# Query packing from PSUM, a transferred key copy and a joined value product in a hybrid decoder step

## The chip, the cores and the metric

One Trainium2 chip; the kernel runs on one of its cores. The metric is the device time of one execution in microseconds (us), as the median of several runs. An execution is also recorded by the hardware profiler; its trace gives every instruction's start and duration on the engines: PE (TensorE matmul), PEld (its weight loads), DVE (VectorE), ACT (ScalarE), POOL (GpSimd) and SP (SyncE, which issues the DMA transfers here).

## The reference, cut to what matters

One inference step of a decoder trunk: dilated sliding-window attention (layer 0 here), a pooling mixer, and a gated convolution feed-forward after each. The change touches the attention of the 1024 prompt tokens only. There are three groups of 16 heads with dilation 1, 4 and 16; in each residue stream a query attends to itself and the 128 keys before it.

```python
def banded_attention(q, k, v, bias):
    ...
    s = jnp.einsum("nbqhd,nbkhd->nbhqk", qb, kb).astype(jnp.float32) * SCALE
    s = s + bias[:, np.clip(rel, 0, SPAN)]
    s = jnp.where(valid[None, :, None], s, NEG_INF)
    m = jnp.max(s, axis=-1)
    p = jnp.exp(s - m[..., None])
    l = jnp.sum(p, axis=-1)
    o = jnp.einsum("nbhqk,nbkhd->nbqhd", p.astype(v.dtype), vb).astype(jnp.float32)
```

All of it is float32. The kernel gets there with the float32r matmul: each operand is split into a high part (rounded to float32r) and a low part (the rest), and a product is the sum of high by high, high by low and low by high.

## The kernel before, in words

The attention stage works through 24 units, `order` (L794): head pair `hp` 0 to 7, and in each the groups `g` 2 (dilation 16), 1, 0. A unit's projection is 9 groups of 24 matmuls of 336 to 352 columns (3 operands `which` = q, k, v by 3 token chunks `c`), `accumulate` (L111). They are written to two PSUM banks in turn (tile `mm`, `bufs=2`), and `evacuate` (L356) empties a bank with one ACT instruction (L364) into the tile `raw` (tag `raw`, 3 buffers: q, k, v), in the order of the group's residue streams, so that for g of 1 and 2 the writes are strided.

While unit n is projected, the attention of unit n-1 is worked off beside it. `attend` (L803) puts its steps on a list with due places on a `clock` that ticks once per 3 matmuls (`between`, L834), 72 ticks to a unit: `scores` i at 6i+1, `probs_t` i at 6i+15, `pv` i at 6i+24, `finish_o` at 6i+26 for odd i, `transpose_v` at 4 and 28. Everything that is due is issued at once, to queues that each engine works off strictly in order. Extra tasks come along every 6 ticks: `Merge` (weights of the three groups, `weights` L558 and `rows` L575) and `Sample` (the 8 sample tokens; its cache loads and POOL products).

Two packing steps prepare scores of the unit under projection. `pack_q` (L386, at ticks 29, 32, 44.5, 46.5) fills the tiles `queries` for two heads h: high part on the head's own 64 partitions, low part on the other 64. `pack_k` (L400, at ticks 50, 53, 56, 59) fills `keys`: high part on both halves of the partitions, low part on the own half. Head 0 uses ACT and POOL, head 1 DVE alone, for the queries; for the keys DVE makes the own copy (L404), ACT the other (L405), and POOL or DVE the low part (L406). A score is then one product of `queries` with each of the two planes of `keys`.

`probs_t` transposes the probabilities into the PSUM bank `pt` (1 buffer), ACT takes the high part (L475) and DVE the low part (L476) into `phl`. `pv_mm` (L479) multiplies: for each head, `v` high and low side by side (128 stationary columns) by the high, then by the low probabilities (L485), four matmuls of 128 columns per step for g = 2, accumulated in one bank of tile `o` (3 buffers). ACT (L504) brings one half of the partitions over, DVE (L521) adds the halves.

Weights for every stage are 128x1024 tiles that are split by ACT (L95) and POOL (L96). After the attention stage a projection and two feed-forward layers follow; the change does not touch them, nor the norm code, but the norm's tiles at the start (`place`, L295) share the tag `p` with the probabilities.

Of the kernel before, what the change touches and what calls it, by code (L numbers as in the profile page):

```python
# [18 lines left out]
T, NS = 1024, 8  # L19
# [8 lines left out]
TAB = 384  # L28
RAW = 3

# [15 lines left out]
def trunk(ctx: ExitStack, tc: tile.TileContext, a, out):  # L46
# [231 lines left out]
    with ExitStack() as ph:  # L278
        qp = ph.enter_context(tc.tile_pool(name="qkv", bufs=1))
        mmp = ph.enter_context(tc.tile_pool(name="mmp", bufs=1, space=PSUM))  # L280
        app = ph.enter_context(tc.tile_pool(name="app", bufs=1, space=PSUM))
        sample_cols = [qp.tile([128, 3, 8, NS], F32, name=f"{x}s") for x in "qkv"]
        units = {}
# [4 lines left out]
        keys = [qp.tile([128, 2, T], F32R, name=f"k{h}") for h in range(2)]  # L288

        def load_x(c):  # L290
            c0, c1 = CHUNKS[c]
            for k in range(8):
                nc.sync.dma_start(out=xT[k][:, c0:c1], in_=a["x"][:, k, c0:c1])

        def place(kind, j=0, c=0):  # L295
            if kind in ("row", "square"):
                return qp.tile([128, 512], F32, name="nrow", tag="p", bufs=4)
            if kind == "acc":
                return part[:, j, CHUNKS[c][0]:CHUNKS[c][1]]
# [24 lines left out]
        def tables():  # L324

            def step(g, tag, src):
# [6 lines left out]
                else:  # L333
                    bs = qp.tile([16, 512], F32, name="bs", tag="p", bufs=4)[:, :136]
                    nc.vector.tensor_copy(bs, ps)
# [20 lines left out]
        def evacuate(u, which, ps, c):  # L356
# [24 lines left out]

        A, B = slice(0, 64), slice(64, 128)

        queries = []

        def pack_q(u):  # L386

            raw = u.raw[0]
            if not queries:
                queries.extend(x_row(h, F32R)[:, :T] for h in range(2))  # L390
# [7 lines left out]
            return parts(part, (0, T // 2))  # L398
# [12 lines left out]

        def parts(f, starts):
            return [partial(f, h, own, other, slice(t, t + T // 2)) for t in starts
                    for h, (own, other) in enumerate(((A, B), (B, A)))]

# [16 lines left out]
        def transpose_v(u, half):  # L432
            ps = app.tile([128, 4, 2, 64], F32, name="vt", tag="misc")
            for j in range(4):
                i = 4 * half + j
                nc.tensor.transpose(ps[:, j].rearrange("p a d -> p (a d)"),  # L436
                                    u.raw[2][:, T - 128 * i - 128:T - 128 * i], ident)
            v = qp.tile([128, 4, 2, 128], F32R, name="vhl", tag="vhl", bufs=2)
            nc.scalar.activation(v[:, :, :, 0:64], ps, AF.Copy)
            nc.vector.tensor_sub(v[:, :, :, 64:128], ps, v[:, :, :, 0:64].bitcast(F32))  # L440
            u.v[half] = v

        def scores(u, i):
# [3 lines left out]
            ps = app.tile([128, 2, 2, 128], F32, name="s", tag="s")  # L447
            p = qp.tile([128, 2, 256], F32, name="p", tag="p", bufs=4)
            if w == 128:
                for h in range(2):  # L450
                    nc.tensor.matmul(ps[:, h], queries[h][:, q], keys[h][:, :, k], start=True, stop=True)  # L451
                nc.vector.tensor_add(p[:, :, :w], ps[:, :, 0], u.bias[:, :, :w])
                s, bias = ps[:, :, 1], p
            else:
                s, bias = ps.rearrange("p h a q -> p h (a q)"), u.bias
                for h in range(2):
                    for x in range(2):
                        nc.tensor.matmul(s[:, h], queries[h][:, q], keys[h][:, x, k], start=x == 0, stop=x == 1)  # L458
            for h in range(2):
# [29 lines left out]
        def pv(u, j):  # L489
            first = j % 2 == 0  # L490
            if first:
                u.o = app.tile([128, 2, 256], F32, name="o", tag="o", bufs=3)
                if j and u.pt[j - 1][1] == 256:
# [3 lines left out]
            if j % 2:  # L497

                x = 256 * (j // 2 % 2)
                tmp = (part[:, 0, x:x + 256] if (u.hp, u.g) != order[23] else  # L500
                       qp.tile([128, 256], F32, name="ot", tag="ot", bufs=1))
                u.tmp = tmp, u.o
                for h, (own, other) in enumerate(((A, B), (B, A))):
                    nc.scalar.activation(tmp[own], u.o[other, h], AF.Copy)  # L504

        def finish_o(u, i):
# [13 lines left out]
            for h, own in enumerate((A, B)):  # L520
                nc.vector.tensor_add(dst[own], split(o[own, h]), split(tmp[own]))  # L521

# [17 lines left out]
        class Merge:  # L540
# [43 lines left out]
            def fetch(self, g):  # L584
                if self.hp < 7:
                    cb = x_row(2)[:, :T]
                else:
                    cb = qp.tile([128, NT], F32, name="cb", tag="raw", bufs=RAW)[:, :T]
                self.cb[g] = cb
# [307 lines left out]
        for n, (hp, g) in enumerate(order):  # L897
# [9 lines left out]
            for i, (which, c) in enumerate(seq):  # L907
                if which == len(wt):
                    wt.append(None if (n, i) == (0, 2) else w_get())
                    u.raw.append(qp.tile([128, NT], F32, name="raw", tag="raw", bufs=RAW))  # L910
                    if n:
# [38 lines left out]
                if i == 6 and n:  # L950
                    load_bias(u)
                if n and i in (2, 5):
                    places = (29, 29 + 3, 44.5, 44.5 + 2) if i == 2 else [50 + 3 * j for j in range(4)]
                    plan.extend(zip(places, pack_q(u) if i == 2 else pack_k(u)))
                    plan.sort(key=lambda x: x[0])
                if n == 0 and i == 5:
                    for f in tables() + [partial(load_bias, u)]:
                        later(f, .8)
                if n == 0 and i in (6, 7):
                    nc.scalar.activation(warm, ones, AF.Exp)  # L960
                    for f in pack_q(u) if i == 6 else pack_k(u):
                        later(f, .6)
# [461 lines left out]
```

## Time and profile before

| | us |
|---|---|
| median of 3 runs | 2929.45 (2928.8 to 2935.96) |
| the profiled execution | 2928.91 |
| its span, first to last instruction | 2927.1 |
| PE busy in the span | 2790.0 (95%) |
| DVE / ACT / POOL busy | 1510.3 / 1240.5 / 1165.0 |
| DMA moved | 227.41 MB |

Matmuls are pipelined and their ends are modelled, so PE's work is best read from the distance between the starts of neighbouring matmuls. Idle time of an engine is put down to what released it. The stretch from 75 to 1180 us holds units 1 to 23, each with the attention of the unit before it; the last unit's attention runs beside the output projection up to about 1260 us.

### The profile page before, as it was taken

How to read it: one execution, taken by the hardware profiler on the slowest of the kernel's cores; microseconds unless marked ns; L12 is line 12 of the kernel's file. 1: busy time of each engine (PE TensorE's matmuls, PEld its weight loads, DVE VectorE, ACT ScalarE, POOL GpSimd, SP SyncE). 2: the span in 40 equal slices, each digit the busy share in tenths (PEclk: the TensorE clock that was granted, in tenths of full speed). 3: DMA queues.
4: the chain of work that ended last, by engine and by line, in shares of the span. 5: the costliest groups of instructions: out<-in, count | busy, mean ns of one | idle time of the engine just before them, and what ended most of it. 6: DMA issues, size and time to landing. Idle time of an engine off the chain costs nothing.

```text
span 2927.1 us, 45930 instructions
## 1 busy us (share of the span) xinstructions
PE 2790.0 (95%) x18109; PEld 2742.4 (94%) x18109; DVE 1510.3 (52%) x3146; ACT 1240.5 (42%) x2596; POOL 1165.0 (40%) x853
## 2 busy tenths in 40 slices
PE   6999999999999999999999999997797999999998
PEld 5999999999999999889999999997797999999998
DVE  6566666666676657663322223248986322222235
ACT  5565665666565656434221213134444231222222
POOL 4235443544354535454323323255544332323321
PEclk9999999999999999999999999999898999999999
DMA  3134323432343235526111111133327211111111
GB/s 118 55 92 117 106 73 94 114 111 68 97 123 101 68 99 153 143 78 72 44 51 44 51 44 45 50 95 100 90 68 88 66 50 44 51 44 51 44 44 61
DMA packets 190119, 227.41 MB, mean 78 GB/s; under 512 B 68736, under 2 KB 152560, under 8 KB 189904
## 3 DMA queue, kind: packets, MB, share of 16 engines
q1 hardware_dynamic: 189856, 224.47, 28.5%
q8 instruction: 142, 2.33, 0.3%
q14 instruction: 73, 0.60, 0.1%
q10 hardware_dynamic: 48, 0.02, 0.0%
HBM read 201.55 MB, written 23.34 MB: 77 GB/s over the span
## 4 chain that ended last, share of the span: by engine, by line
PE 78%; DVE 13%; ACT 3%; issue 3%; DMA 1%; POOL 1%; SPq 0%; DVEq 0%; ACTq 0%; POOLq 0%
PE mm L116 70%; PE o L485 2%; DVE k L404 2%; PE s L458 1%; PE pt L471 1%; DVE sums L1221 1%; DVE x L395 1%; DVE conv L1112 1%; PE s L451 1%; DVE nrow L239 1%; DVE sc L630 1%; DVE x L521 1%; DVE x L393 1%; PE spv L764 1%; PE vt L436 1%
## 5 line engine op out<-in xcount | busy, mean ns | idle before, releaser
L116 PE MATMUL mm<-hh,w_hi 128*128 128x352 f32 (+2 forms) x4064 | 1346.0, 331 | 28.9 <-DVE conv L1103 9.7
L116 PE MATMUL mm<-hh,w_lo 128*128 128x352 f32 (+2 forms) x4064 | 1309.2, 322 | 7.4 <-POOL w_lo L96 7.4
L116 PE MATMUL mm<-hl,w_hi 128*128 128x352 f32 (+2 forms) x4064 | 1309.8, 322 | 4.8 <-DVE hl L251 4.5
L116 PEld LDWEIGHTS mm<-hh,w_hi 128*128 128x128 f32 x4064 | 773.5, 190 | 37.6 <-DVE conv L1103 10.2
L116 PEld LDWEIGHTS mm<-hl,w_hi 128*128 128x128 f32 x4064 | 773.9, 190 | 9.2 <-DVE hl L251 8.4
L116 PEld LDWEIGHTS mm<-hh,w_lo 128*128 128x128 f32 x4064 | 772.2, 190 | 8.8 <-POOL w_lo L96 8.8
L96 POOL TENSOR_TENSOR w_lo<-w_raw,w_hi 128x1024 fp32r<-128x1024 f32 x194 | 478.9, 2470 | 614.1 <-ACT w_hi L95 595.8
L1112 DVE SCALAR_TENSOR_TENSOR conv<-gate,convp,conv 128x1024 f32<-128x1024 f32 (+3 forms) x126 | 134.5, 1068 | 476.9 <-ACT conv L1110 464.6
L116 PE MATMUL mm<-gh,w_hi 128*128 128x352 f32 (+2 forms) x1056 | 339.0, 321 | 7.6 <-ACT gh L1104 7.6
L116 PE MATMUL mm<-gl,w_hi 128*128 128x352 f32 (+2 forms) x1056 | 339.2, 321 | 1.2 <-POOL gl L1105 1.2
L116 PE MATMUL mm<-gh,w_lo 128*128 128x352 f32 (+2 forms) x1056 | 338.7, 321 | 0.2 <-POOL w_lo L96 0.2
L1048 DVE TENSOR_TENSOR x<-x,mm 128x352 f32<-128x352 f32 (+2 forms) x312 | 159.1, 511 | 308.9 <-PE mm L116 308.7
L95 ACT ACTIVATE w_hi<-w_raw 128x1024 fp32r<-128x1024 f32 x196 | 205.5, 1051 | 241.6 <-PE mm L116 231.3
L463 ACT ACTIVATE p<-p,st 128x128 f32<-128x128 f32 (+1 forms) x384 | 169.9, 443 | 204.2 <-DVE st L460 203.6
L1105 POOL TENSOR_TENSOR gl<-conv,gh 128x352 fp32r<-128x352 f32 (+2 forms) x132 | 122.5, 938 | 269.9 <-ACT gh L1104 269.9
L116 PEld LDWEIGHTS mm<-gh,w_hi 128*128 128x128 f32 x1056 | 199.5, 189 | 8.2 <-ACT gh L1104 8.1
L116 PEld LDWEIGHTS mm<-gl,w_hi 128*128 128x128 f32 x1056 | 199.3, 189 | 1.8 <-POOL gl L1105 1.8
L116 PEld LDWEIGHTS mm<-gh,w_lo 128*128 128x128 f32 x1056 | 199.4, 189 | 0.5 <-POOL w_lo L96 0.5
L96 POOL TENSOR_TENSOR w_lo<-part,w_hi 128x1024 fp32r<-128x1024 f32 x56 | 138.2, 2469 | 152.2 <-ACT w_hi L95 144.3
L476 DVE TENSOR_TENSOR phl<-pt,phl 128x512 fp32r<-128x512 f32 (+1 forms) x192 | 104.6, 545 | 165.7 <-ACT phl L475 164.5
L1094 ACT ACTIVATE gate<-mm 128x352 f32<-128x352 f32 (+2 forms) x132 | 60.0, 455 | 302.7 <-PE mm L116 302.5
L364 ACT ACTIVATE raw<-mm 128x336 f32<-128x336 f32 (+1 forms) x216 | 144.6, 670 | 101.1 <-PE mm L116 97.7
(192 smaller groups left out, 3260.9 us busy)
## 6 DMA issues: line engine op xcount, KB each, us to landing
w_raw<-in_w_in SPq DMA_DIRECT2D x76, 512.0 KB
w_raw<-in_w_qkv SPq DMA_DIRECT2D x72, 512.0 KB
part<-in_w_in SPq DMA_DIRECT2D x38, 512.0 KB
w_raw<-in_w_out SPq DMA_DIRECT2D x36, 512.0 KB
x<-qd SPq DMA_DIRECT2D x48, 256.0 KB
kc<-in_cache_k SPq DMA_DIRECT2D x48, 256.0 KB
vc<-in_cache_v SPq DMA_DIRECT2D x48, 256.0 KB
x<-c_d SPq DMA_DIRECT2D x42, 256.0 KB
```

The source lines that it names most:

```text
L95: nc.scalar.activation(hi, raw, AF.Copy)
L96: (eng or nc.gpsimd).tensor_sub(lo, raw, hi.bitcast(F32))
L116: nc.tensor.matmul(ps, l, r, start=first and i == 0, stop=last and i == n - 1)
L364: nc.scalar.activation(stream(raw[:, :T], u.g, c0, t1, which > 0), ps[:, :w].rearrange("p (s r) -> p s r", r=DILS[u.g]), AF.Copy, scale=si ...
L404: nc.vector.tensor_copy(keys[h][own, 0, t], raw[own, t])
L463: nc.scalar.activation(p[:, h, :w], p[:, h, :w], AF.Exp, bias=u.st[:, i, h, 0:1], scale=-1.0, accum_out=u.st[:, i, h, 1:2])
L476: nc.vector.tensor_sub(phl[:, :, 1, :w], ps[:, :, :w], phl[:, :, 0, :w].bitcast(F32))
L485: nc.tensor.matmul(u.o[:, h, 128 * q:128 * (q + b1 - b0)], u.v[j // 4][:, j % 4, h, :], u.pt[j][0][:, h, x, 128 * b0:128 * b1], start=firs ...
L1048: nc.vector.tensor_add(xT[ct][:, c0:c1], xT[ct][:, c0:c1], ps)
L1094: nc.scalar.activation(gate[:, 2 + s:2 + e], group(tiles8(w, c), c), AF.Copy)
L1105: nc.gpsimd.tensor_sub(self.gl[f][:, s:e], conv[:, s:e], self.gh[f][:, s:e].bitcast(F32))
L1112: nc.vector.scalar_tensor_tensor(conv[:, c0:t1], gate[:, j + c0:j + t1], cw[j], conv[:, c0:t1], op0=ALU.mult, op1=ALU.add)
```

## The change

- **Queries.** `evacuate` for q no longer writes `raw`. For each head, ACT writes the high part from PSUM into the query tile (64 partitions), and DVE subtracts it from the same PSUM columns with one scalar_tensor_tensor into the other 64 partitions. `pack_q` is gone. There are two sets of query tiles: the rows x0 and x1 for odd units as before, and a new pair `other_queries` for even ones.
- **Keys.** `pack_k` works in two halves of the tokens, at ticks 50 and 54: two ACT copies to the own partitions, the two low parts on POOL and DVE as before. The copy on the other 64 partitions is made by two transfers from SP (128 KB each) at ticks 53 and 57, in place of an ACT copy; the own copy moves from DVE to ACT.
- **Values.** The high and low parts of v are laid out so that the high part sits on the head's own partitions. For g = 2 one matmul per head of 256 columns multiplies by the high and the low probabilities together, into a bank of its own per head; the sum is now made by an ACT copy, one more DVE addition per head and the final DVE addition.
- **Room.** `raw` has 2 buffers, `p` 3, the tile `ot` takes a `bias` buffer, one of the last merge's `cb` tiles a `phl` buffer.

```diff
-RAW = 3
+RAW = 2
...
+        other_queries = [qp.tile([128, T], F32R, name=f"q{h}") for h in range(2)]
+        queries = []
...
-                return qp.tile([128, 512], F32, name="nrow", tag="p", bufs=4)
+                return qp.tile([128, 512], F32, name="nrow", tag="p", bufs=3)
...
-            sign = -1.0 if which == 0 else 1.0
-            nc.scalar.activation(stream(raw[:, :T], u.g, c0, t1, which > 0),
-                                 ps[:, :w].rearrange("p (s r) -> p s r", r=DILS[u.g]), AF.Copy, scale=sign * scale)
+            src = ps[:, :w].rearrange("p (s r) -> p s r", r=DILS[u.g])
+            if which == 0:
+                for h, (own, other) in enumerate(((A, B), (B, A))):
+                    hi, lo = (stream(raw[h][x], u.g, c0, t1, False) for x in (own, other))
+                    nc.scalar.activation(hi, src[own], AF.Copy, scale=-scale)
+                    nc.vector.scalar_tensor_tensor(lo, src[own], -scale, hi.bitcast(F32), op0=ALU.mult, op1=ALU.subtract)
+            else:
+                nc.scalar.activation(stream(raw[:, :T], u.g, c0, t1, True), src, AF.Copy)
...
-        def pack_q(u):
-            raw = u.raw[0]
...
-            def part(h, own, other, t):
-                (nc.vector.tensor_copy(queries[h][own, t], raw[own, t]) if h else
-                 nc.scalar.activation(queries[h][own, t], raw[own, t], AF.Copy))
-                (nc.vector if h else nc.gpsimd).tensor_sub(queries[h][other, t], raw[own, t],
-                                                           queries[h][own, t].bitcast(F32))
...
         def pack_k(u):
             raw = u.raw[1]
-            def part(h, own, other, t):
-                nc.vector.tensor_copy(keys[h][own, 0, t], raw[own, t])
-                nc.scalar.activation(keys[h][other, 0, t], raw[own, t], AF.Copy)
-                (nc.vector if h else nc.gpsimd).tensor_sub(keys[h][own, 1, t], raw[own, t],
-                                                           keys[h][own, 0, t].bitcast(F32))
-            return parts(part, (T // 2, 0))
+            def part(t):
+                for h, own in enumerate((A, B)):
+                    nc.scalar.activation(keys[h][own, 0, t], raw[own, t], AF.Copy)
+                for h, own in enumerate((A, B)):
+                    (nc.vector if h else nc.gpsimd).tensor_sub(keys[h][own, 1, t], raw[own, t],
+                                                               keys[h][own, 0, t].bitcast(F32))
+            def twice(t):
+                for h, (own, other) in enumerate(((A, B), (B, A))):
+                    nc.sync.dma_start(out=keys[h][other, 0, t].bitcast(F32), in_=keys[h][own, 0, t].bitcast(F32))
+            return [partial(f, slice(t, t + T // 2)) for t in (T // 2, 0) for f in (part, twice)]
...
-            v = qp.tile([128, 4, 2, 128], F32R, name="vhl", tag="vhl", bufs=2)
-            nc.scalar.activation(v[:, :, :, 0:64], ps, AF.Copy)
-            nc.vector.tensor_sub(v[:, :, :, 64:128], ps, v[:, :, :, 0:64].bitcast(F32))
-            u.v[half] = v
+            v = qp.tile([128, 4, 4, 64], F32R, name="vhl", tag="vhl", bufs=2)
+            hi, lo = v[:, :, 0:4:3], v[:, :, 1:3]
+            nc.scalar.activation(hi, ps, AF.Copy)
+            nc.vector.tensor_sub(lo, ps, hi.bitcast(F32))
...
-            p = qp.tile([128, 2, 256], F32, name="p", tag="p", bufs=4)
+            p = qp.tile([128, 2, 256], F32, name="p", tag="p", bufs=3)
...
+            if u.g == 2:
+                for h in range(2):
+                    nc.tensor.matmul(u.o[h][:, :, 128 * q:128 * q + 128], u.v[j // 4][:, j % 4, h, :],
+                                     u.pt[j][0][:, h, :, 0:128], start=first, stop=True, skip_group_check=True)
+                return
...
-                u.o = app.tile([128, 2, 256], F32, name="o", tag="o", bufs=3)
+                if u.g == 2:
+                    u.o = [app.tile([128, 2, 256], F32, name="o", tag="o", bufs=3) for _ in range(2)]
+                else:
+                    u.o = app.tile([128, 2, 256], F32, name="o", tag="o", bufs=3)
...
-                    nc.scalar.activation(tmp[own], u.o[other, h], AF.Copy)
+                    if u.g == 2:
+                        nc.scalar.activation(tmp[own], u.o[h][other, 0], AF.Copy)
+                        nc.vector.tensor_add(tmp[own], u.o[h][own, 1], tmp[own])
+                    else:
+                        nc.scalar.activation(tmp[own], u.o[other, h], AF.Copy)
...
-                if n and i in (2, 5):
-                    places = (29, 29 + 3, 44.5, 44.5 + 2) if i == 2 else [50 + 3 * j for j in range(4)]
-                    plan.extend(zip(places, pack_q(u) if i == 2 else pack_k(u)))
+                if n and i == 5:
+                    plan.extend(zip((50, 53, 54, 57), pack_k(u)))
                     plan.sort(key=lambda x: x[0])
...
-                if n == 0 and i in (6, 7):
+                if n == 0 and i == 7:
                     nc.scalar.activation(warm, ones, AF.Exp)
-                    for f in pack_q(u) if i == 6 else pack_k(u):
+                    for f in pack_k(u):
                         later(f, .6)
```

## Rows read from the trace of the kernel before

**Rows 1.** Attention stage: its us; busy us of PE, PEld, DVE, ACT, POOL; clock; DMA.

```profile
75.00:1180.00 1105.00, 1066.85 (x7309) 1043.67 (x7308) 716.48 (x1850) 661.12 (x1671) 501.05 (x298) 0.99 0.35 98
```

**Rows 2.** Waits of PE from 75 to 1180 us: total, times, longest.

```profile
PE o L485 <- DVE phl L476: 10.7, 8, 1.9
PE pt L471 <- DVE phl L476: 9.4, 15, 0.9
PE mt L578 <- DVE me L573: 8.3, 4, 2.2
```

**Rows 3.** Timeline of PE around a value product of group 2: start, duration, instruction.

```profile
375.70 0.56 PE L485 MATMUL o<-phl,vhl 128*128 128x128 f32 x4
376.09 0.37 PE L116 MATMUL mm<-hh,w_hi 128*128 128x352 f32 x1
376.30 0.32 PE L116 MATMUL mm<-hl,w_hi 128*128 128x352 f32 x1
...
376.62 0.40 PE L451 MATMUL s<-k,x 128*128 128x256 f32 x2
376.86 0.33 PE L116 MATMUL mm<-hh,w_hi 128*128 128x352 f32 x1
377.02 0.32 PE L116 MATMUL mm<-hl,w_hi 128*128 128x352 f32 x1
```

**Rows 4.** Timelines of POOL, DVE and PE before a wait, 247 to 255 us.

```profile
247.21 2.44 POOL L96 TENSOR_TENSOR w_lo<-w_raw,w_hi 128x1024 fp32r<-128x1024 f32 x1
...
247.78 2.17 DVE L404 CAST k<-raw 64x512 fp32r<-64x512 f32 x1
...
254.81 0.55 PE L485 MATMUL o<-phl,vhl 128*128 128x128 f32 x3 [1.87 <-DVE phl L476]
```

**Rows 5.** DVE groups by shape, 60 to 1235 us: busy us, mean ns.

```profile
L404 DVE CAST k<-raw 64x512 fp32r<-64x512 f32 x96 | 104.8, 1092 | 2.2
...
L395 DVE TENSOR_TENSOR x<-raw,x 64x512 fp32r<-64x512 f32 x48 | 44.7, 932 | 1.6
...
L393 DVE CAST x<-raw 64x512 fp32r<-64x512 f32 x48 | 37.2, 774 | 0.8
```

**Rows 6.** Single lines: count, shortest, median and longest ns, first and last start.

```profile
L364 ACT ACTIVATE raw<-mm x216: 426/760/832, 28.1 to 1175.1; 128x336 f32<-128x336 f32 x72, 128x352 f32<-128x352 f32 x36
L395 DVE TENSOR_TENSOR x<-raw,x x48: 686/687/2767, 65.7 to 1161.3; 64x512 fp32r<-64x512 f32 x48
L521 DVE TENSOR_TENSOR x<-o,part x184: 404/603/637, 95.9 to 1178.0; 64x256 f32<-64x256 f32 x184
L476 DVE TENSOR_TENSOR phl<-pt,phl x192: 407/425/694, 86.3 to 1223.8; 128x256 fp32r<-128x256 f32 x104, 128x512 fp32r<-128x512 f32 x88
```

**Rows 7.** Timelines of PE and ACT, unit 4: one query bank filled, emptied, due again.

```profile
220.10 0.32 PE L116 MATMUL mm<-hh,w_lo 128*128 128x336 f32 x1
...
221.11 0.75 ACT L364 ACTIVATE raw<-mm 128x336 f32<-128x336 f32 x1
...
224.70 0.32 PE L116 MATMUL mm<-hh,w_hi 128*128 128x352 f32 x1
```

**Rows 8.** Timelines of ACT and PE as unit 1 begins.

```profile
68.81 1.94 ACT L405 ACTIVATE k<-raw 64x512 fp32r<-64x512 f32 x3
...
73.64 0.38 PE L451 MATMUL s<-k,x 128*128 128x256 f32 x1 [2.91 <-POOL k L406]
```

**Rows 9.** Timelines of SP and POOL: two 256 KB transfers and their reader.

```profile
506.25 1.30 SPq L592 DMA_DIRECT2D x<-c_d  x2
...
511.57 2.40 POOL L598 TENSOR_TENSOR x<-x,x 128x1024 f32<-128x1024 f32 x1 [5.20 <-DMA x<-c_d]
```

**Rows 10.** Timeline of POOL at the start: one low part of the norm.

```profile
17.25 0.94 POOL L251 TENSOR_TENSOR hl<-nrow,hh 128x352 fp32r<-128x352 f32 x1 [2.83 <-ACT hh L247]
```

**Rows 11.** Timelines of DVE and ACT in the last attention.

```profile
1189.42 1.23 DVE L847 TENSOR_TENSOR hl<-at,hh 128x1024 fp32r<-128x1024 f32 x1 [1.72 <-ACT hh L846]
...
1193.83 1.05 ACT L846 ACTIVATE hh<-at 128x1024 fp32r<-128x1024 f32 x1
```

More of the change, by code (lines that the diff above doesn't have):

```diff
@@ L281, in trunk @@
         app = ph.enter_context(tc.tile_pool(name="app", bufs=1, space=PSUM))
+        A, B = slice(0, 64), slice(64, 128)
         sample_cols = [qp.tile([128, 3, 8, NS], F32, name=f"{x}s") for x in "qkv"]
@@ L333, in step @@
                 else:
-                    bs = qp.tile([16, 512], F32, name="bs", tag="p", bufs=4)[:, :136]
+                    bs = qp.tile([16, 512], F32, name="bs", tag="p", bufs=3)[:, :136]
                     nc.vector.tensor_copy(bs, ps)
@@ L437, in transpose_v @@
                                     u.raw[2][:, T - 128 * i - 128:T - 128 * i], ident)
-            v = qp.tile([128, 4, 2, 128], F32R, name="vhl", tag="vhl", bufs=2)
-            nc.scalar.activation(v[:, :, :, 0:64], ps, AF.Copy)
-            nc.vector.tensor_sub(v[:, :, :, 64:128], ps, v[:, :, :, 0:64].bitcast(F32))
-            u.v[half] = v
+            v = qp.tile([128, 4, 4, 64], F32R, name="vhl", tag="vhl", bufs=2)
+            hi, lo = v[:, :, 0:4:3], v[:, :, 1:3]
+            nc.scalar.activation(hi, ps, AF.Copy)
+            nc.vector.tensor_sub(lo, ps, hi.bitcast(F32))
+            u.v[half] = v.rearrange("p j x d -> p j (x d)").rearrange("p j (h e) -> p j h e", h=2)
         def scores(u, i):
@@ L447, in scores @@
             ps = app.tile([128, 2, 2, 128], F32, name="s", tag="s")
-            p = qp.tile([128, 2, 256], F32, name="p", tag="p", bufs=4)
+            p = qp.tile([128, 2, 256], F32, name="p", tag="p", bufs=3)
             if w == 128:
                 for h in range(2):
-                    nc.tensor.matmul(ps[:, h], queries[h][:, q], keys[h][:, :, k], start=True, stop=True)
+                    nc.tensor.matmul(ps[:, h], u.raw[0][h][:, q], keys[h][:, :, k], start=True, stop=True)
                 nc.vector.tensor_add(p[:, :, :w], ps[:, :, 0], u.bias[:, :, :w])
@@ L457, in scores @@
                     for x in range(2):
-                        nc.tensor.matmul(s[:, h], queries[h][:, q], keys[h][:, x, k], start=x == 0, stop=x == 1)
+                        nc.tensor.matmul(s[:, h], u.raw[0][h][:, q], keys[h][:, x, k], start=x == 0, stop=x == 1)
             for h in range(2):
@@ L500, in pv @@
                 tmp = (part[:, 0, x:x + 256] if (u.hp, u.g) != order[23] else
-                       qp.tile([128, 256], F32, name="ot", tag="ot", bufs=1))
+                       qp.tile([128, 2, 256], F32, name="ot", tag="bias", bufs=2)[:, 0])
                 u.tmp = tmp, u.o
                 for h, (own, other) in enumerate(((A, B), (B, A))):
-                    nc.scalar.activation(tmp[own], u.o[other, h], AF.Copy)
+                    if u.g == 2:
[3 more added lines that the diff above has]
+                        nc.scalar.activation(tmp[own], u.o[other, h], AF.Copy)
         def finish_o(u, i):
@@ L520, in finish_o @@
             for h, own in enumerate((A, B)):
-                nc.vector.tensor_add(dst[own], split(o[own, h]), split(tmp[own]))
+                nc.vector.tensor_add(dst[own], split(o[h][own, 0] if u.g == 2 else o[own, h]), split(tmp[own]))
         stat_d = {}
@@ L586, in fetch @@
                     cb = x_row(2)[:, :T]
+                elif g:
+                    cb = qp.tile([128, NT], F32, name="cb", tag="raw", bufs=RAW)[:, :T]
                 else:
-                    cb = qp.tile([128, NT], F32, name="cb", tag="raw", bufs=RAW)[:, :T]
+                    cb = qp.tile([128, T], F32, name="cb", tag="phl", bufs=2)
                 self.cb[g] = cb
@@ L909, in trunk @@
                     wt.append(None if (n, i) == (0, 2) else w_get())
-                    u.raw.append(qp.tile([128, NT], F32, name="raw", tag="raw", bufs=RAW))
+                    if which:
+                        u.raw.append(qp.tile([128, NT], F32, name="raw", tag="raw", bufs=RAW))
+                    elif n % 2:
+                        if not queries:
+                            queries.extend(x_row(x, F32R)[:, :T] for x in range(2))
+                        u.raw.append(queries)
+                    else:
+                        u.raw.append(other_queries)
                     if n:
```

8 lines of the change are left out of this document (removed).

## Prediction, made before the changed kernel was run

> **What bounds the kernel now.** I read the busy time by stage first. [...]
>
> The waits of PE say what it stands for: 10.7 us before value products and 9.4 us before transposes, both for DVE's low part of the probabilities, and 8.3 us for DVE's merge weights, 28.4 us together [rows 2]. The timelines before such a wait show why DVE is late: a cast of the key packing, a plain SBUF copy, began at 247.78, beside a POOL subtraction that ran until 249.65, and took 2.17 us; later in the same queue stood the low part that PE waited 1.87 us for [rows 4]. The casts take 1092 ns in the mean for keys, 774 for queries, the DVE subtractions of queries 932 [rows 5], and those subtractions go from 687 ns in the median up to 2767. The subtraction with a PSUM operand never needs more than 694 ns in 192 times [rows 6]. So what is late on DVE are instructions that read SBUF alone, beside POOL.
>
> **Part by part: value product.** Four matmuls of 128 columns start at 375.70, the next projection matmul at 376.09 and its successor at 376.30: 0.60 us. Two matmuls of 256 columns, in the score beside it, take from 376.62 to 377.02 for the same: 0.40 us [rows 3]. That is the form the change brings to group 2: 8 units of 8 steps, 64 times 0.20 us = 12.8 us off PE's own work. The slower successor may not be due to the four (0.21 against 0.16 us); without it 64 x 0.15 = 9.6 us is the lower bound. Nothing hides or returns this, since PE is the bound.
>
> **Waits for DVE.** Gone from DVE are the key casts and its query packing: 104.8 + 44.7 + 37.2 = 186.7 us [rows 5]. New are 144 subtractions of about 344 columns from PSUM and 64 additions. A DVE instruction from PSUM costs 425 ns at 256 columns and 690 at 512 [rows 6], 1.04 ns a column, so 0.51 us at 344; a strided output adds (637 - 404) / 256 = 0.91 ns a column [rows 6], so 0.82 us for groups 1 and 2. If the strided second input costs as much again it is 1.13 us, the upper bound. I take 0.82 because the strided row is an addition with a PSUM operand, as here. The new work is 96 x 0.82 + 48 x 0.51 + 64 x 0.41 = 129 us: DVE loses 58 us, and what comes instead stands in the first third of a unit, not around ticks 44 to 59 where the waits arise. POOL loses its query subtractions too. The key subtractions stay on DVE and still meet POOL. I take three quarters of the 28.4 us, 21.3; bounds 8 and 28.4.
>
> [...]
>
> **Emptying the query banks.** Before, one ACT instruction emptied a bank: the last matmul began at 220.10, ACT started at 221.11 for 0.75 us, and the bank was due again at 224.70, so 2.8 us were spare [rows 7]. Now the bank is free only after ACT, DVE, ACT, DVE. In strict order, with 0.05 us for each hand-over, that is 1.01 + 2 x 0.75 + 2 x 0.82 + 0.2 = 4.35 us against 4.60: it just fits. With 1.13 us it is 4.97 and PE stands 0.4 us. ACT halves its partitions but not its time, and while it waits for DVE its queue holds: the exponentials, the high parts of the probabilities and the next bank. In group 0, where ACT needs 426 ns [rows 6], there is room. Bounds: nothing, and 0.8 us at two chunks of 16 units, 25 us; I take 7 (0.1 us for each of 72), near the lower end because the likelier price of DVE fits.
>
> **PSUM banks of the value product.** Group 2 now holds two of the three banks per pair of steps, and the next pair needs one back 4 ticks after `finish_o`. A tick is 1105 / 23 / 72 = 0.67 us, so 2.7 us for two additions of 0.6 us behind the new one. 24 such places; bounds 0 and 5 us (0.2 each), taken 1.
>
> **Key copy by transfer.** SP issues it at tick 53, and the first score reads it at tick 73: 13 us. Two 256 KB transfers were issued at 506.25 and their reader started at 511.57 [rows 9], 5.3 us, so it is hidden, behind SP's earlier loads too if these hold SP for less than 8 us. The wait on ACT's copy also holds SP's later loads by some us; the weights are due a whole operand later. Bounds 0 and 10, taken 1. Only unit 1 has no such room: the ACT copies start at 68.81 and take 0.65 each, so two are done at 70.1, the transfers at about 75.4, where the score now starts at 73.64 [rows 8]; +1.5, bounds -1 and 4. The own copies that ACT takes over replace those that the transfer takes away.
>
> **Buffers.** With three `p` tiles the norm at the start may wait for a POOL subtraction of 0.94 us [rows 10] before a tile is free; up to five such, 0 to 5 us, taken 2. In the last attention the second `at` load can start only when DVE has read the first, at 1190.65; 512 KB take about 5.3 us [rows 9], so ACT's reader comes at 1196 instead of 1193.83 [rows 11] and holds the exponentials: 0 to 4, taken 1.5. The `raw`, `ot` and `cb` moves fall where the former holder is done, nothing.
>
> **The sum.** The profiled execution took 2928.91 us, 0.5 under the median. 2928.9 - 12.8 - 21.3 + 7 + 1 + 1 + 1.5 + 2 + 1.5 = 2908.8; on the median's scale 2909.
>
> **Rivals.** *Query banks become the bound* (slower). If DVE needs 1.13 us and ACT comes a further 1 us late because its queue was held for the bank before, the chain is 6.0 us against 4.6: 1.4 us at two chunks of 16 units, 45 us. 2928.9 - 34.1 + 45 + 7 = 2947. It decides from 0.95 us per subtraction, or from 0.25 us more delay on ACT. For it: little is spare, ACT is at 60%. Against: the third chunk has more room and lets ACT catch up. Chance 0.12.
>
> *DVE stays late.* The key subtractions beside POOL alone keep PE waiting, and only 5 of the 28.4 us come back: 2928.9 - 12.8 - 5 + 14 = 2925. For it: two of them may still cost over 1.2 us. Against: the sum of what stood in the queue before the wait was mostly casts [rows 4]. Chance 0.17.
>
> *Key copy late.* SP held for 8 us or more in most units: 23 starts by 0.7 us, 16 us more than forecast: 2925. The change then fails at what it moves. Chance 0.06.
>
> *Everything fits.* If ACT may read the second head's half of the bank while DVE reads the first, the chain is 1.01 + 0.75 + 0.75 + 0.05 + 0.82 = 3.4 us, the banks cost nothing, all 28.4 us return, and half of the small prices fall away: 2928.9 - 12.8 - 28.4 + 4 = 2892. Nothing in the trace shows whether the two reads are kept apart. Chance 0.15. [...]
>
> **How the numbers follow.** The forecast has 0.50. A measurement of this kernel can tell 0.3%, 9 us, from no change. Below 2920.7: the forecast but for its upper edge and the last rival, 0.64. Within 9 us: that edge, the second and third rival, 0.23. Above 2938: the first, 0.13. The range takes in the last rival with a little below it and the unknown prices up to 2934, and leaves out the first.
>
> **What would show it.** Right, if in the new profile the waits of PE for the low part of the probabilities and the merge weights fall from 28 to under 10 us, the product of group 2 takes 0.24 us to its successor, and waits of projection matmuls for the query subtraction stay under 10 us. The step on DVE is wrong if the new subtraction is above 0.95 us, the step on transfers if scores wait for a DMA beyond unit 1, the forecast if PE's waits in the stage don't fall below 38 us.

## The result and the profile after

The changed kernel takes 3003.77 us (median; 2998.73 to 3005.15) against 2929.18 us: a ratio of 1.0246, 95% interval 1.0227 to 1.0265. Forecast were 2909 us, range 2888 to 2934. The profiled execution has a span of 3003.1 us against 2927.1.

I split the span at the first projection matmul of each unit, read from PE's timeline, and sum the units by the group whose attention runs beside them:

| us | before | after | |
|---|---|---|---|
| start, up to unit 1 | 69.6 | 83.2 | +13.6 |
| 8 units beside attention of group 2 | 376.1 | 420.6 | +44.5 |
| 8 units beside group 1 | 355.2 | 359.3 | +4.1 |
| 7 units beside group 0 | 374.0 | 390.0 | +16.0 |
| unit 23's end to the end of the span | 1752.2 | 1750.1 | -2.1 |

The stages after answer to [rows 1] (columns as there; the second row is units 1 to 23, which before took 1105.3 us):

```profile
0.00:83.20 83.20, 55.15 (x262) 46.10 (x263) 43.26 (x83) 41.14 (x79) 25.71 (x29) 0.90 0.29 92
83.20:1253.00 1169.80, 1075.11 (x7170) 1040.26 (x7170) 677.02 (x1864) 689.91 (x1695) 440.04 (x252) 0.98 0.38 104
```

DVE and POOL have less to do, as meant, and the stage is 64.5 us longer all the same: PE stands for 95 us, where before it stood for 38 (1105.00 less 1066.85, [rows 1]). The granted clock has a part in it too: it was 0.50 for 48 us of these units, before for 14, and 1.00 in the rest (last section). PE's waits after, from 75 to 1255 us, beside [rows 2]:

```profile
PE qr L678 <- DVE qs L377: 19.3, 12, 2.2
PE pt L467 <- DVE phl L472: 18.6, 21, 1.2
PE o L482 <- DVE x L530: 17.1, 9, 3.1
PE s L447 <- DVE st L456: 10.2, 8, 1.4
PE spv L775 <- DVE so L802: 8.2, 6, 2.2
PE s L447 <- DMA k<-k: 5.5, 1, 5.5
...
PE s L454 <- DVE st L456: 3.7, 4, 0.9
...
PE o L487 <- DVE phl L472: 0.4, 1, 0.4
```

The waits that were to go are gone in two of three cases: value products for the low part (10.7 to 0.4 us) and the merge weights (8.3 us, no longer in the list). Those of transposes (`pt`) have doubled, 9.4 to 18.6 us. New are waits for DVE of the sample query `qr`, of scores and of value banks. No projection matmul of these units waits for a query bank.

What a score waits for shows in unit 4, timelines of ACT, DVE and PE (start, duration, instruction, and in brackets the idle time before it):

```profile
239.90 0.79 ACT L372 ACTIVATE q<-mm 64x352 fp32r<-64x352 f32 x1 [0.86 <-PE mm L116]
241.56 0.81 ACT L372 ACTIVATE q<-mm 64x352 fp32r<-64x352 f32 x1 [0.86 <-DVE q L373]
...
240.73 0.79 DVE L373 SCALAR_TENSOR_TENSOR q<-mm,q 64x352 fp32r<-64x352 f32 x1 [0.96 <-ACT q L372]
242.40 0.78 DVE L373 SCALAR_TENSOR_TENSOR q<-mm,q 64x352 fp32r<-64x352 f32 x1 [0.87 <-ACT q L372]
243.21 0.42 DVE L448 TENSOR_TENSOR p<-s,bias 128x256 f32<-128x256 f32 x1
243.67 0.29 DVE L456 CUSTOM_DVE_ANT_0 p<-s,p 128x128 f32<-128x128 f32 x1
...
244.32 0.48 PE L447 MATMUL s<-k,x 128*128 128x256 f32 x2 [1.45 <-DVE st L456]
```

The bank is empty 3.28 us after ACT began (239.90 to 243.18), where one ACT instruction did it before [rows 7]; that is in time. But the score of 239.70 is issued right behind the evacuation, so its bias addition (L448) stands behind both subtractions in DVE's queue and starts at 243.21, though DVE stood idle for 0.87 us in between. There is one score bank; the next score needs it and stands 1.45 us. This is no single case. Followed back along DVE's queue, all waits of sample queries (19.3 us) and of scores (13.9) and 12.2 of the 18.6 us of transposes end in a short DVE instruction that ran right behind a query subtraction, and that one had itself waited for ACT: 45 of the 95 us.

The start has the same pattern with the norms, and the clock on top. ACT waited 3.21 us before the second half of the first query bank, because DVE had norm work ahead of its first subtraction; ACT's later work slid with it, and PE stood twice, where before it had 1.1 us of such waits there:

```profile
33.81 0.79 ACT L372 ACTIVATE q<-mm 64x352 fp32r<-64x352 f32 x1 [3.21 <-DVE q L373]
...
46.13 0.65 PE L116 MATMUL mm<-hh 128*128 128x336 f32 x1 [6.05 <-ACT raw L375]
...
62.88 0.42 PE L116 MATMUL mm<-hh,w_hi 128*128 128x344 f32 x1 [2.31 <-ACT raw L375]
```

Windows of the same kernel (columns as in [rows 1]) show a granted clock of 0.50 beside or soon after each of the two waits:

```profile
45.00:50.00 5.00, 3.87 (x14) 3.87 (x15) 1.13 (x2) 1.67 (x4) 1.21 (x2) 0.50 0.00 0
55.00:60.00 5.00, 5.00 (x35) 5.00 (x34) 4.73 (x10) 3.26 (x8) 2.83 (x4) 1.00 0.00 0
65.00:70.00 5.00, 5.00 (x16) 3.54 (x16) 0.83 (x2) 0.38 (x1) 0.00 (x0) 0.50 0.03 7
70.00:75.00 5.00, 5.00 (x16) 3.19 (x14) 1.57 (x3) 0.95 (x2) 0.00 (x0) 0.53 0.04 10
```

And a value bank of group 2 comes late, DVE and PE in unit 4:

```profile
273.84 1.23 DVE L401 TENSOR_TENSOR k<-raw,k 64x512 fp32r<-64x512 f32 x1 [1.71 <-ACT k L399]
...
275.44 0.86 DVE L511 TENSOR_TENSOR part<-o,part 64x256 f32<-64x256 f32 x2
276.37 1.52 DVE L401 TENSOR_TENSOR k<-raw,k 64x512 fp32r<-64x512 f32 x1
277.90 0.75 DVE L641 TENSOR_REDUCE sc<-kc 128x4 f32<-128x256 f32 x2
278.68 1.22 DVE L530 TENSOR_TENSOR x<-o,part 64x256 f32<-64x256 f32 x2
...
279.41 0.48 PE L482 MATMUL o<-phl,vhl 128*128 128x256 f32 x1 [1.89 <-DVE x L530]
```

The final additions (L530), which free two of three banks, stand behind a key subtraction and the sample's reductions. A key subtraction stands there in eight of the nine such waits, 15.9 of 17.1 us. The wait shown ended beside a fall of the clock; PE, busy all through the 3.4 us after it, began 13 matmuls there at a granted clock of 0.50, those of 336 columns 0.28 us apart (columns as in [rows 1]):

```profile
279.50:282.90 3.40, 3.40 (x13) 3.40 (x14) 1.48 (x4) 0.45 (x1) 2.45 (x3) 0.50 1.05 360
```

### The profile page after: what moved, and what is told of

Read it like the earlier page. It is cut to its first block, busy times and chain, and to the rows that moved or that the text cites. A ratio compares the mean times of both kernels' runs of the same rounds, so it can differ in the third digit from the quotient of the medians.

```text
span 3003.1 us, 45930 instructions
## 1 busy us (share of the span) xinstructions
PE 2807.1 (93%) x17981; PEld 2747.8 (91%) x17981; DVE 1471.4 (49%) x3162; ACT 1269.1 (42%) x2619; POOL 1100.7 (37%) x805
## 3 DMA queue, kind: packets, MB, share of 16 engines
q8 instruction: 141, 2.31, 0.3%
## 4 chain that ended last, share of the span: by engine, by line
PE 53%; DVE 8%; ACT 3%; issue 1%; DMA 1%; POOL 1%; DVEq 0%; ACTq 0%; SPq 0%; POOLq 0%
PE mm L116 51%; DVE sums L1238 1%; DVE conv L1129 1%; DVE part L211 1%; DMA w_raw<-in_w_in 1%; DVE nrow L239 1%; PE o L487 0%; ACT w_hi L95 0%; DVE hl L251 0%; DVE hl L1273 0%; POOL w_lo L96 0%; DVE x L1065 0%; ACT p L459 0%; PE s L454 0%; DVE x L373 0%
## 5 line engine op out<-in xcount | busy, mean ns | idle before, releaser
L375 ACT ACTIVATE raw<-mm 128x352 f32<-128x352 f32 (+1 forms) x144 | 96.8, 674 | 109.6 <-PE mm L116 108.4
```

Source lines behind the costliest of these rows:

```text
L375: nc.scalar.activation(stream(raw[:, :T], u.g, c0, t1, True), src, AF.Copy)
```

## The experiments

Theory A: the query evacuation holds DVE's and ACT's queues. Theory B: the loss comes from group 2's value banks and additions. The first four kernels put one or two of the three parts (queries Q, keys K, values V) alone. All times are medians, with the ratio to the kernel before and its 95% interval.

**Queries alone** (K, as in the diff, and V of the kernel after put back to before; room and buffers as after):

```
-            return [partial(f, slice(t, t + T // 2)) for t in (T // 2, 0) for f in (part, twice)]
+            return parts(part, (T // 2, 0))
```

> The kernel after, with the key packing and the value product of before put back: what stays is the query packing from PSUM, with the smaller buffers. Theory A (the query evacuation ACT, DVE, ACT, DVE holds the queues of both engines, so that scores, transposes and the start come late behind it): the start keeps its 13 us, the waits in the first third of a unit stay, and the old waits for the low part of the probabilities are partly gone; 2965 to 2985 us, most of the loss of the kernel after. Theory B (the loss comes from group 2's two value banks and the extra additions on DVE): below 2945 us, the start aside.

2985.27 us, 1.0198 (1.0183 to 1.0214). The start is 83.0 us long, the units beside group 2 cost 18.5 us, group 1 5.6, group 0 18.5 more than before. Theory A, just beyond its upper end.

**Values alone:**

```
+            if u.g == 2:
+                for h in range(2):
+                    nc.tensor.matmul(u.o[h][:, :, 128 * q:128 * q + 128], u.v[j // 4][:, j % 4, h, :],
+                                     u.pt[j][0][:, h, :, 0:128], start=first, stop=True, skip_group_check=True)
+                return
```

> The kernel before with the joined value product of group 2 alone. PE's own work falls by about 1.0 us in each of 8 units. Theory A: the banks of the value product wait little, 2918 to 2926 us. Theory B: waits for a free value bank of 2 us and more in most of the 8 units eat the gain, 2935 us or more.

2946.54 us, 1.0071 (1.0051 to 1.0090). Theory B holds for this part: PE's own time from group 2's products to the next matmul falls from 26.1 to 18.8 us, and to the one after that from 39.6 to 29.9 (starts of neighbouring matmuls, waits left out), but the waits (68 to 1255 us) rise:

```profile
PE o L487 <- DVE x L535: 22.0, 8, 4.3
PE pt L473 <- DVE phl L478: 19.9, 18, 2.8
```

**Keys alone:**

```
-                nc.vector.tensor_copy(keys[h][own, 0, t], raw[own, t])
-                nc.scalar.activation(keys[h][other, 0, t], raw[own, t], AF.Copy)
+                    nc.scalar.activation(keys[h][own, 0, t], raw[own, t], AF.Copy)
...
+                    nc.sync.dma_start(out=keys[h][other, 0, t].bitcast(F32), in_=keys[h][own, 0, t].bitcast(F32))
```

> The kernel before with the key copy by transfer alone (own copies on ACT, no casts on DVE). Theory A: PE's waits for the low part of the probabilities (20 us) and for the merge weights (8 us) mostly go, unit 1 loses 2 to 5 us to the transfer: 2905 to 2917 us. Rival: DVE stays late behind the key subtractions beside POOL, or SP or ACT come late: 2925 us or more.

2909.74 us, 0.9941 (0.9926 to 0.9956): a gain of 17 us, the fastest kernel but for a variant that can't be told from it. Its waits, same window:

```profile
PE pt L477 <- DVE phl L482: 13.1, 15, 1.3
PE spv L770 <- DVE so L797: 9.7, 8, 2.2
PE s L457 <- DMA k<-k: 4.1, 1, 4.1
```

**Keys and values:**

> The kernel after with the old query packing and the old buffers: key copy by transfer and joined value product together. Theory A: the two gains add up, 2897 to 2912 us, and the kernel after minus this one, about 95 us, is the price of the query packing. Theory B: value banks that come late behind DVE cost 15 us or more, 2920 us or more.

2928.22 us, 1.0004 (0.9995 to 1.0013), the two edits above together. Here my theory A was wrong: the value product is no gain but eats what the keys give. By the ratios Q costs 58, V 21, K gives 17; the sum is 62 of the 72 us that the kernel after loses. About 10 us come only with all three together, which is as much as the four intervals leave open; where they arise was not tried.

**What in V costs.** Two banks without the additions (each head's four products of 128 columns go to a bank of its own), and the additions without the banks:

```
+                    u.o = [app.tile([128, 2, 256], F32, name="o", tag="o", bufs=3) for _ in range(2)]
```

```
+                    if u.g == 2:
+                        nc.vector.tensor_add(part[own, 0, 512 + x:768 + x], u.o[own, h], tmp[own])
```

> The kernel before, in which group 2's four products of 128 columns stay as they are but each head has a bank of its own, two of three per pair of steps; no addition more. If the number of banks is what costs in the joined value product (22 us of waits for a free value bank there): those waits return, 8 to 20 us more than before, 2935 to 2947 us. If the extra additions on DVE are what costs: no measurable change, 2924 to 2930 us.

> The kernel before with two more DVE additions per pair of steps in group 2, of the joined product's shape and at its place, into a place that nobody reads; products and banks as before. If the additions cost by making the low part of the probabilities and all behind it late on DVE: 8 us or more, 2935 us or more, as longer waits for the low part. If the banks are the cause: within 5 us of before.

Banks: 2940.48 us, 1.0035 (1.0024 to 1.0045), with 14.4 us of waits for banks, all behind a key subtraction on DVE. (Its profile is of the fastest execution, 2931.13 us; units 1 to 23 are 9.6 us longer in it than before.) Additions: 2944.38 us, 1.0047 (1.0030 to 1.0063), and other waits grow:

```profile
PE pt L471 <- DVE phl L476: 15.1, 18, 1.8
...
PE mm L116 <- ACT raw L364: 8.2, 5, 1.9
PE o L485 <- DVE phl L476: 6.6, 9, 1.5
```

Both cost, 10 and 14 us. For the additions the waits grow by 9 us in all, and the clock is 0.50 for 34 us of units 1 to 23, before for 14 (over the whole span it is 0.981, before 0.984). With 10 to 13 us less work on PE the two make 11 to 14 of V's 21 us; the rest is not accounted for, and the intervals are 3 to 6 us wide either way.

**Room alone** (`p` with 3 tiles):

> The kernel before with three tiles p in place of four. Theory A (the query evacuation delays the start): at most 3 us more, 2926 to 2930 us, unit 1 begins at 70 to 72 us. Rival (the smaller room delays the start): unit 1 begins at 80 us or later and the time is 2937 us or more.

2932.47 us, 1.0010 (1.0000 to 1.0019); unit 1 begins at 71.7 us, 2.1 later. The room is not what delays the start.

**Order of the evacuation.** On queries alone, first ACT, ACT, DVE, DVE:

```
-                for h, (own, other) in enumerate(((A, B), (B, A))):
-                    hi, lo = (stream(raw[h][x], u.g, c0, t1, False) for x in (own, other))
...
+                for f in range(2):
+                    for h, (own, other) in enumerate(((A, B), (B, A))):
...
+                        if f == 0:
+                            nc.scalar.activation(hi, src[own], AF.Copy, scale=-scale)
+                        else:
+                            nc.vector.scalar_tensor_tensor(lo, src[own], -scale, hi.bitcast(F32), op0=ALU.mult, op1=ALU.subtract)
```

> The query packing alone (2985 us) with the evacuation's four steps issued as ACT, ACT, DVE, DVE: the same instructions on the same bank, no ACT instruction stands behind a DVE one. Theory A (the alternation holds both queues for 3.3 us): the start loses its 13 us nearly, and half of the waits in a unit's first third go, 2945 to 2965 us. Rival (the load itself, 144 subtractions of 0.75 us and the second ACT instruction, is what costs): 2978 us or more.

2970.24 us, 1.0138 (1.0123 to 1.0153). Neither theory: 18 us come back by the ratios, 11 in the profiled executions, 6.6 of these at the start; but the waits of the units stay nearly whole (scores beside group 2: 10.8 us, 11.2 before this edit). So the alternation is not what makes the units' waits; it has a part in the start. DVE still waits at the head of its queue for ACT, with the score's steps behind it. Theory A, new: what counts is what stands behind the subtractions on DVE.

Then the two subtractions a tick later, behind the score's steps, and the sample columns read ahead (`low` does the two subtractions, `LATE` is 1; unit 0 as in the kernel above):

```
+                    plan.append((clock[0] + LATE, low))
```

> The query packing with ACT, ACT, DVE, DVE (2970 us), its two DVE subtractions issued one tick later, behind the DVE work of the score that is due with the evacuation, and the sample columns read ahead of both; first unit as it was. Theory A, in its new form (the score's DVE steps stand behind the subtractions in DVE's queue, and the one score bank, the transposes and the sample query come late from there): the waits of scores for DVE (15 us), of sample queries (18 us) and half of those of transposes (10 us) go, 2935 to 2950 us. Rival (it is the time of the bank or the load of ACT and DVE, whatever the order): the waits turn into waits of projection matmuls for the bank, 2965 us or more.

2968.85 us, 1.0143 (1.0128 to 1.0158): a miss in the total. The waits for scores went (15 to 0.9 us), as did those of transposes (10 to 0.8) and two thirds of those of the sample query, and one of 21.2 us came in their place; waits and the timeline of DVE and PE in unit 4:

```profile
PE vt L439 <- DVE qr_sb L675: 21.2, 12, 2.4
```

```profile
239.84 0.15 DVE L368 TENSOR_SCALAR qs<-mm 128x8 f32<-128x8 f32 x1
241.60 1.49 DVE L379 SCALAR_TENSOR_TENSOR q<-mm,q 64x336 fp32r<-64x336 f32 x2 [1.61 <-ACT q L375]
243.13 0.42 DVE L455 TENSOR_TENSOR p<-s,bias 128x256 f32<-128x256 f32 x1
...
244.01 0.27 DVE L675 COPY qr_sb<-qr 16x128 f32<-16x128 f32 x1
...
244.34 0.66 PE L439 MATMUL vt<-consts,raw 128*128 128x128 f32 x4 [2.35 <-DVE qr_sb L675]
```

In the third chunk a copy of 0.27 us, which frees the bank that `vt` needs, stands behind subtractions that themselves wait 1.61 us for ACT. The same edit with the key transfers:

> The kernel after without the joined value product and with the later subtractions: key transfers and query packing from PSUM together. Theory A: the later query packing costs 8 to 23 us over before, of it about 7 at the start, the key transfers give 17 back: 2918 to 2933 us. If query packing without the queue's harm is a gain in itself, beside ACT's and POOL's lighter load: below 2910 us, the fastest kernel here.

2971.9 us, 1.0158 (1.0141 to 1.0175): both theories missed; the transfers give nothing here, and the wait of `vt` is 21.2 us as above.

Now only the third chunk's subtractions two ticks later still (`LATE` is 1, 1, 3 by chunk):

```
-                    plan.append((clock[0] + LATE, low))
+                    plan.append((clock[0] + LATE[c], low))
```

> The later subtractions (2969 us) with those of the third chunk two ticks later still, so that the scores of that place and the copy of the sample query (whose wait took 21 us) stand ahead of them on DVE. If what stands behind the subtractions in DVE's queue is the cause: those 21 us go and nothing of that size takes their place, 2945 to 2954 us, of which the start keeps about 10. If it is the length of the chain or the load, whatever the order: the wait moves once more, to the bank or to the next reader, 2960 us or more.

2932.71 us, 1.0007 (0.9996 to 1.0019): below the range that I gave, by the ratios 40 us less than with one tick, by moving a third of the subtractions past a few short instructions. The wait is gone without a substitute; the copy now runs first, and `vt` starts on time:

```profile
234.44 0.28 DVE L675 COPY qr_sb<-qr 16x128 f32<-16x128 f32 x1
235.27 1.56 DVE L379 SCALAR_TENSOR_TENSOR q<-mm,q 64x336 fp32r<-64x336 f32 x2 [0.55 <-ACT q L375]
...
235.50 0.60 PE L439 MATMUL vt<-consts,raw 128*128 128x128 f32 x4
```

The same instructions cost 58 us in one order and 2 in another. What remains is the start (unit 1 at 77.5 us); the units beside group 2 take 4.6 us less than before.

> The same with the key transfers (2972 us before this edit). Queue order as the cause: 2935 to 2955 us, by the wait of the sample query less than 2972. Load as the cause: 2962 us or more.

2934.04 us, 1.0013 (1.0002 to 1.0023), just below the range for the queue order. With Q in good order the waits that K was to remove are gone already (transposes 0.8, value products 2.6 us in the kernel above), and K pays for unit 1's transfer: its first score waits 6.7 us, where it waits 0.7 in the kernel above.

**The kernel after itself, only the order changed:**

> The kernel after itself with one thing changed: the evacuation's order ACT, ACT and the two DVE subtractions later (one, one and three ticks by chunk). If DVE's queue order is the larger cause in the kernel after as well, the 15 us that the joined value product still costs over the same kernel without it stay, and 2945 to 2960 us come out, 45 us or more below the 3003 of the kernel after. If the loss of the kernel after is not of that kind, 2985 us or more.

2946.21 us, 1.0058 (1.0042 to 1.0075), in the range that I gave for the queue order: by the ratios 55 of the 72 us come back. In units 1 to 23 of the profiles, 52 us shorter, PE's waits fall from 94 to 52 us, and the time at a clock of 0.50 from 48 to 31 us (over the whole span the clock is 0.980, in the kernel after 0.976). What stays is V (15.5 us of waits for its banks) and the start (82.8 us). So the order of the evacuation is the larger cause in the kernel after too. This edit changes it on both queues, ACT's and DVE's; only on queries alone were the two taken apart, and there DVE's later places gave 40 of the 56 us.

**Two variants of keys alone.** Unit 0's key copies by ACT, and the query packing's DVE cast on ACT:

```
+                    if u is units[order[0]]:
+                        nc.scalar.activation(keys[h][other, 0, t], raw[own, t], AF.Copy)
...
-                (nc.vector.tensor_copy(queries[h][own, t], raw[own, t]) if h else
+                nc.scalar.activation(queries[h][own, t], raw[own, t], AF.Copy)
```

> The kernel before with the key copies by transfer in all units but the first, where ACT copies instead (2910 us with transfers in all). If the 4 us that unit 1's first score waits for the transfer are on the path, 2905 to 2908 us; if ACT's copies there bring another wait of the same size, 2909 to 2911 us.

> The key transfers alone (2910 us) with the DVE cast of the query packing also on ACT, so that DVE has 37 us less in the stretch where transposes wait 13 us for the low part of the probabilities. If DVE's queue is what these wait for: 2900 to 2907 us. If ACT, which is then the busier of the two, delays its own high parts: 2909 us or more.

2908.52 us, 0.9938 (0.9923 to 0.9953), not to be told from 2909.74: instead of 4.1 us for the transfer PE waits 3.2 us for key subtractions, as the kernel before does. And 2920.03 us, 0.9974 (0.9963 to 0.9986), a miss: less work on DVE, and yet transposes wait 17.5 us for its low part where they waited 13.1. It is not that ACT's high parts come late, as the rival had it. In all 20 of these waits the low part ran behind a DVE key subtraction, mostly of 1.8 to 1.9 us, and 17 of the 20 subtractions had themselves waited 0.5 to 1.6 us for ACT's key copies: the pattern of the query subtraction again.

## Why the prediction was wrong

**The step that failed** is the sentence on DVE's new work: that it "stands in the first third of a unit, not around ticks 44 to 59 where the waits arise". Waits arise where something long stands ahead of something short that frees the only bank; before, the first third of units 1 to 23 had 4.5 us of PE's 39 us of waits, and nothing long stood there. After, the three thirds have 37.7, 24.8 and 31.9 us, where before they had 4.5, 5.1 and 29.8; the third chunk's subtractions fall at the start of the middle third. I counted DVE's busy time (which fell, 717 to 677 us, by 40 where I took 58) and the bank's time, and not what is queued behind the subtractions. For ACT I named the queue and priced it at nothing; for DVE I did not ask. Queries alone cost 58 us where I took 7 for the bank, bounds 0 and 25, and 2 for the room; with only the order changed they cost 2. The clock stood nowhere in the sum either: it fell beside the waits, which is an estimate of up to 17 us of the 64.5 in units 1 to 23 (last section).

**Emptying the query banks** was right in that the banks did not become the bound: no projection matmul of units 1 to 23 waited for one, where I took 7 us. A subtraction takes 0.76 us in groups 1 and 2 and 0.51 in group 0, never above 0.81 (I took 0.82 and 0.51, upper end 1.13), and the chain of 3.28 us fits; its three hand-overs took 0.03 to 0.04 us (I took 0.05), and ACT needed 0.79 and 0.81 us for 64 partitions of 352 columns, where it had needed 0.75 for 128 of 336 [rows 7]. The two reads of a bank came one after the other: ACT's second half waited for DVE's first all 72 times, 58.5 us together, 0.86 in the case shown. Whether both could read at once no run here shows. So the premise of the rival "everything fits" was out, though the bank costs nothing as it said.

**The start** was left out of that step. Unit 0's evacuations share DVE and ACT with the norms: 13.6 us, of which the room (`p`, I took 2) is 2.1. With ACT, ACT, DVE, DVE PE's waits for ACT there fall from 8.4 us to 4.3 to 6.8 in six kernels; in the kernel after, all of PE's waits up to unit 1 are 8 us longer than before, and the time at a clock of 0.50 (17 us of it, before 3) is an estimate of up to 7 us more, half of the difference. How much of it goes with the order was not taken apart (last section).

**Value product.** The form behaves as foreseen, two matmuls and 0.24 us to the successor:

```profile
251.92 0.40 PE L482 MATMUL o<-phl,vhl 128*128 128x256 f32 x2
252.16 0.33 PE L116 MATMUL mm<-hh,w_hi 128*128 128x352 f32 x1
```

Counted as I had counted it, to the start of the second matmul behind, it takes 11.0 us off PE's own work (39.6 to 28.6), between my 9.6 and 12.8; in the 58 of 64 steps that lie wholly at a clock of 1.00 the step fell from 0.62 to 0.42 us, the 0.20 that I took. What was wrong is "Nothing hides or returns this", though PE was busy for 1066.85 of 1105.00 us before [rows 1]: the banks, priced at 1 us (0 to 5), cost 10, because the additions that free them stand behind a key subtraction and not alone as I assumed; the 64 additions, 0.42 us each, cost 14 where I saw only DVE's sum.

**Waits for DVE.** Right in kind and nearly in size: I took 21.3 us back, bounds 8 and 28.4; the keys alone gave 17. That the key casts are what was late holds for the value products (10.7 to 0.7 us) and the merge weights (8.3 us, gone). It does not hold for the transposes: with the casts gone they wait 13.1 us, before 9.4, each time right behind a key or query subtraction. For them the rival that DVE stays late was right, and its counter-argument was weak: of the 7.7 us of DVE work from 246.65 to 254.33, before the wait of [rows 4], 3.7 were casts, not most of it.

**Key copy by transfer.** Hidden as foreseen, except unit 1, whose first score waits 5.5 us in the kernel after and 4.1 alone. My 1.5, bounds -1 and 4, was the delay over before, where that score waited too, 2.9 us for a key subtraction [rows 8]. Counted from the unit's start the score begins 1.2 us later with the keys alone and 2.5 later in the kernel after: the term was right.

**Buffers and tail.** `p` costs 3 us by its ratio (lower end 0), which agrees with 2; the 1.5 us at the tail don't show, the rest of the span is 2.1 us shorter.

**The rivals.** The slower side came, at a chance of 0.13, but not by its rival: no query bank became the bound, and 3004 us lie far above its 2947. The sign to look for that I gave last was the right one: PE's waits did not fall below 38 us.

## What to carry to other kernels

When an instruction is added that waits for another engine, list what is queued behind it on its own engine up to its end, and for each the bank or buffer that it frees and how many of them there are; the busy share of the engine says nothing of this. Place such an instruction behind the short ones that free a single bank, and as late as its own bank allows: here the order, with both high parts ahead on ACT and the subtractions later on DVE, was worth 56 us for the query packing, 40 of them by the last move on DVE alone, and 55 in the whole kernel. Read the granted clock along with the waits: beside eleven of them it fell to 0.50 here, by an estimate up to 17 us more than before (last section). A change of three parts is worth taking apart: the one part that paid, the keys, had its 17 us hidden behind two that cost.

## What was not expected of the hardware

After waits of PE of 6.05 and 2.31 us in the start the granted clock was 0.50 in the windows 45 to 50 and 65 to 70 us, 1.00 from 55 to 60, and still 0.53 from 70 to 75. In the attention stage it fell beside shorter waits too, down to 1.0 us. In units 1 to 23 of the kernel after it fell to 0.50 eleven times, each time beside a wait of PE of 1.0 to 5.5 us, for 48 us together; before, four times for 14 us. At 0.50 matmuls of 336 columns began 0.28 us apart (279.69 to 282.21 us), at 1.00 they began 0.15 us apart (239.94 to 242.56), so nearly half of such a time is lost. Half of the difference is an estimate of its cost: up to 17 us, less where PE stood anyway. With 55 us more of waits and about 13 us less work on PE that makes 59 of the 64.5 us. Over the whole span the clock was 0.975 to 0.980 in the executions of the kernel after, and 0.980 to 0.987 in those of the kernel before. Beside other waits it stayed up: in the kernel after it was 1.00 from 200 to 210 us, around one of 1.71 us that ended at 203.36, and no run here shows what decides it.

And a like start doesn't always get a like clock: the two kernels with three ticks for the third chunk, on queries alone and in the kernel after, issue nearly the same work for unit 0, and from 45 to 60 and 60 to 75 us they show, first on queries alone, then in the kernel after,

```profile
45.00:60.00 15.00, 14.60 (x84) 14.41 (x84) 7.35 (x18) 6.36 (x14) 3.90 (x5) 0.81 0.00 0
60.00:75.00 15.00, 13.46 (x70) 9.45 (x69) 6.86 (x13) 7.50 (x11) 1.00 (x4) 1.00 0.07 11
```

```profile
45.00:60.00 15.00, 12.92 (x88) 12.60 (x89) 8.72 (x21) 8.74 (x17) 5.04 (x8) 1.00 0.01 1
60.00:75.00 15.00, 15.00 (x43) 8.88 (x43) 4.46 (x9) 4.47 (x6) 0.00 (x0) 0.53 0.02 6
```

a clock of 0.81 and then 1.00 in one, 1.00 and then 0.53 in the other. Unit 1 begins at 77.5 us in the first and at 82.8 in the second. The first had the longer waits for ACT before that (6.8 us, the longest 5.2; the second 5.2 and 3.6), and yet less time at 0.50: by these windows 5.7 us, the second 14.1. Half of the difference, 4 us, is an estimate of what the clock alone makes of the 5.3 between the two starts, and single profiles of a start are not to be compared closer than that.
